# A hybrid attention and delta-rule layer on one core: when the second half's input block is prepared, and how the diagonal blocks travel

## The chip, the cores and the metric

The kernel runs on one core of one Trainium2 chip. Its engines are TensorE (PE, with its weight loads PEld), VectorE (DVE), ScalarE (ACT), GpSimd (POOL) and SyncE (SP), whose queue issues the kernel's DMA transfers. Each engine works through its own list of instructions in order. The metric is the device time of one execution in microseconds; three runs of the kernel before took 1336.61, 1340.53 and 1341.32 us, with the median 1340.53.

## The reference, cut to what matters

One layer takes x (2048 positions of 1024 numbers), normalises it, projects it once, and gives the columns to two groups: a gated delta rule that scans the sequence in both directions (4 heads of 128, chunks of 64) and attention in a band of 128 positions to either side (8 query heads over 2 key/value heads of 64). The outputs are concatenated, projected and added to x.

```python
h = rms_norm(x, norm_w[l])
proj = h @ w_in[l]
(dn_q, dn_k, dn_v, dn_z, dn_beta, dn_decay,
 sw_q, sw_k, sw_v, sw_z) = jnp.split(proj, cuts, axis=-1)
dn = gated_deltanet_bidir(dn_q, dn_k, dn_v, dn_beta, dn_decay,
                          dn_conv_w[l], dn_a_log[l], dn_dt_bias[l])
dn = rms_norm(dn, dn_out_norm_w[l]).reshape(b, s, DN_WIDTH)
dn = dn * jax.nn.silu(dn_z)
sw = windowed_gqa_with_sinks(sw_q, sw_k, sw_v, ...)
sw = sw * jax.nn.silu(sw_z)
x = x + jnp.concatenate([dn, sw], axis=-1) @ w_out[l]
```

Inside the delta rule each chunk needs the inverse of a unit lower triangular matrix:

```python
m = jnp.where(strict, jnp.einsum('bhncd,bhnsd->bhncs', k_beta, k) * decay, 0.0)
eye = jnp.eye(c, dtype=q.dtype)
t_inv = lax.linalg.triangular_solve(eye + m, jnp.broadcast_to(eye, m.shape),
                                    left_side=True, lower=True, unit_diagonal=True)
u = jnp.einsum('bhncs,bhnse->bhnce', t_inv, v * beta[..., None])
w = jnp.einsum('bhncs,bhnsd->bhncd', t_inv, k_beta * jnp.exp(g)[..., None])
def step(state, inp):
    v_new = u_i - jnp.einsum('bhcd,bhde->bhce', w_i, state)
    ...
```

## The kernel before, in words

The sequence is cut into 16 chunks of 128 positions, and into four blocks of 512, two to a half. A float32 product is made of three products of rounded parts (xhi, xlo for the input; wh, wl for a weight).

**Phase A** goes through the two halves. In each half it prepares the input blocks (`xprep` L145 to L165 writes xhi and xlo, whose tiles have two buffers: the second half's first block, xhi2, takes the buffers of the first half's first block), then projects keys, values and queries of the attention (`proj_seq` L191, tiles pq), the gates (`gate_pairs` L202, tiles pf_z, twice 128 channels at a time), and the channels of the delta rule with their convolution (`conv_pair` L217, tiles pf_c: ACT makes the first tap at L233, DVE the other four at L237). Between these pieces of projection it does the attention of one chunk after the other (`attend` L327): PE scores s (L339, L340), DVE the masked maximum (L341), ACT the exponential (L346), POOL the division (L355), PE transposes (L360), ACT and DVE split the result in two parts (L364, L365), PE multiplies with the values (L367, L368), ACT and DVE put the output together in ot (L371 to L374), POOL multiplies with the gate zc and SP stores it as mix_sw (L375 to L378). ot5_1 is the output of chunk 5, the sixth, for the second key/value head.

**Phase B** begins while the last attention is under way. `out_sw` (L564) projects the attention's part of the output chunk by chunk (pcs, with weights that ACT and DVE split into wohs and wols, L542, L543; xrs is the residual that DVE adds, L561). For each of the four heads h there is `pre_front(h)` (L604), which makes the chunk matrices ma from the keys and stores them in DRAM (m_d, L675) in four groups of four chunks, in the order 1, 2, 0, 3; `pre_back(h)` (L689), which loads the 32 x 32 diagonal blocks of all chunks and both directions into L0 and L (L697, L698; a partition for each block), copies L0 into L (L700), solves them all at once in 31 steps of two instructions on DVE (L705, L709; the result is X), stores X as x_d (L710), reloads it in pieces xc in the layout of the chunk matrices (L718), transposes (xt, L719), copies it to its places on POOL (iv L724 to L728, ma L745) and builds each full inverse by products pi (L733); and `scan(h)` (L759), which steps through the chunks in both directions with kqc loads (L771, four buffers) ahead of it. `out_dn` (L865) projects the second part of the output at the end.

**The order** on each engine isn't the order of the program. `set_order` (L884) builds a graph of the instructions with what each one reads and writes, gives each a cost, and plans a list for every engine by repeated forward and backward list scheduling. Its `gate(before, after)` (L984) adds a node to that graph: everything in `after` is planned behind everything in `before`. A gate puts no wait on the chip; it only changes the lists, and all buffers and semaphores follow from them. Tiles that take turns in a buffer are gated in this way anyhow.

## Time and profile before

| | |
|---|---|
| median of three runs | 1340.53 us |
| the profiled execution | 1339.74 us |
| its span on the core | 1338.0 us |
| mean granted clock of PE | 0.979 |
| first chunk's first scores (s0_0) | 169 us |
| last matmul of the first half's projections (z15_0_1) | 332 us |
| last matmul of the second half's projections (z15_1_1) | 724 us |
| last matmul of out_sw | 893 us |
| last reciprocal blocks stored (x_d of head 3) | 1160 us |

A row of a view by stage has the window, its length, the busy time of each engine with the number of instructions in brackets, then the granted clock of PE, the busy share of the DMA engines, and GB/s. A row of the timeline has its start, its duration, the engine, the line, the operation with out<-in, and in square brackets the idle time before it with what ended it. Rows on DMA issues have count, size, and the median time from issue to landing. In the chain of waits a row is start, duration, engine, tile and line. Tile names stand without their numbers in all of these, so that L0 and L are both L, and which chunk or head a row belongs to follows from its time and its place in the order.

### The profile page before, as it was taken

How to read it: one execution, taken by the hardware profiler on the slowest of the kernel's cores; microseconds unless marked ns; L12 is line 12 of the kernel's file. 1: busy time of each engine (PE TensorE's matmuls, PEld its weight loads, DVE VectorE, ACT ScalarE, POOL GpSimd, SP SyncE). 2: the span in 40 equal slices, each digit the busy share in tenths (PEclk: the TensorE clock that was granted, in tenths of full speed). 3: DMA queues.
4: the chain of work that ended last, by engine and by line, in shares of the span. 5: the costliest groups of instructions: out<-in, count | busy, mean ns of one | idle time of the engine just before them, and what ended most of it. 6: DMA issues, size and time to landing. Idle time of an engine off the chain costs nothing.

```text
span 1338.0 us, 22553 instructions
## 1 busy us (share of the span) xinstructions
PE 1258.0 (94%) x7162; PEld 1072.9 (80%) x7162; DVE 885.6 (66%) x2250; ACT 711.3 (53%) x2105; POOL 484.4 (36%) x868
## 2 busy tenths in 40 slices
PE   5999999999999999999999899998979879898998
PEld 4998878788998888888888687778868769788776
DVE  4423387773632399999987899666885877846433
ACT  5422264332433467666667877229868766466310
POOL 1223032100021235755786755228238155170000
PEclk8999999999999999999999999999979989989999
DMA  7442345244443533222334757968567274333776
GB/s 235 135 140 78 104 161 171 73 135 135 148 121 114 163 102 109 72 93 83 96 120 130 249 185 226 291 209 217 144 184 207 84 212 104 94 104 106 233 241 209
DMA packets 219686, 201.16 MB, mean 150 GB/s; under 512 B 48304, under 2 KB 170800, under 8 KB 219568
## 3 DMA queue, kind: packets, MB, share of 16 engines
q1 hardware_dynamic: 219568, 199.73, 48.8%
q8 instruction: 57, 0.93, 0.3%
q14 instruction: 61, 0.50, 0.1%
HBM read 134.59 MB, written 65.08 MB: 149 GB/s over the span
## 4 chain that ended last, share of the span: by engine, by line
PE 72%; DVE 9%; DMA 5%; ACT 5%; POOL 5%; issue 3%; SPq 0%; DVEq 0%; POOLq 0%; ACTq 0%
PE pf_c L186 6%; PE pf_c L187 6%; PE pf_c L188 5%; PE pf_z L186 4%; PE pf_z L187 4%; PE pf_z L188 4%; PE pi L733 4%; PE pt L360 2%; PE pq_q L197 2%; PE pq_q L199 2%; PE pq_q L198 2%; PE pcd L559 2%; PE pcd L560 2%; PE pcd L558 2%; PE pcs L558 2%
## 5 line engine op out<-in xcount | busy, mean ns | idle before, releaser
L237 DVE SCALAR_TENSOR_TENSOR acc<-pf_c,cw,acc 128x512 f32<-128x512 f32 (+1 forms) x192 | 140.0, 745 | 22.7 <-ACT acc L233 20.9
L186 PE MATMUL pf_c<-xhi,wh_c 128*128 128x512 f32 x384 | 149.3, 401 | 1.9 <-DVE acc L237 1.1
L187 PE MATMUL pf_c<-xlo,wh_c 128*128 128x512 f32 x384 | 150.4, 401 | 0.0
L188 PE MATMUL pf_c<-xhi,wl_c 128*128 128x512 f32 x384 | 148.4, 400 | 0.0
L186 PE MATMUL pf_z<-xhi,wh_z 128*128 128x512 f32 x256 | 91.6, 400 | 0.1
L355 POOL TENSOR_SCALAR pr<-pr,st 128x384 f32<-128x384 f32 (+1 forms) x128 | 83.5, 670 | 22.5 <-DVE st L353 19.0
L187 PE MATMUL pf_z<-xlo,wh_z 128*128 128x512 f32 x256 | 91.0, 397 | 0.0
L346 ACT ACTIVATE pr<-pr,st 128x384 f32<-128x384 f32 (+1 forms) x128 | 76.2, 598 | 27.3 <-DVE st L345 26.7
L188 PE MATMUL pf_z<-xhi,wl_z 128*128 128x512 f32 x256 | 90.3, 396 | 0.0
L186 PEld LDWEIGHTS pf_c<-xhi,wh_c 128*128 128x128 f32 x384 | 72.3, 189 | 17.5 <-DVE acc L237 1.9
L188 PEld LDWEIGHTS pf_c<-xhi,wl_c 128*128 128x128 f32 x384 | 72.0, 188 | 14.6
L187 PEld LDWEIGHTS pf_c<-xlo,wh_c 128*128 128x128 f32 x384 | 72.3, 188 | 13.9
L341 DVE CUSTOM_DVE_ANT_0 pr<-s,mask,sink 128x384 f32<-128x384 f32 (+1 forms) x128 | 72.6, 594 | 6.0 <-PE pt L360 2.5
L360 PE MATMUL pt<-ident,pr 128*128 128x128 f32 x368 | 72.8, 276 | 3.3 <-ACT q L323 1.4
L364 ACT ACTIVATE ph<-pt 128x512 fp32r<-128x512 f32 x92 | 53.4, 594 | 40.2 <-PE pt L360 37.3
L365 DVE TENSOR_TENSOR pl<-pt,ph 128x512 fp32r<-128x512 f32 x92 | 62.5, 684 | 9.1 <-ACT ph L364 7.9
L670 DVE SCALAR_TENSOR_TENSOR ma<-gh,bp,dc 128x256 f32<-128x256 f32 x128 | 56.1, 476 | 17.7 <-PE gh L661 10.0
L787 ACT ACTIVATE yk<-py,ck 128x128 f32<-128x128 f32 x120 | 44.0, 367 | 40.4 <-PE py L782 39.1
L360 PEld LDWEIGHTS pt<-ident,pr 128*128 128x128 f32 x368 | 48.6, 141 | 19.2 <-POOL pr L355 4.8
L178 DVE TENSOR_TENSOR wl_c<-ws_c,wh_c 128x512 fp32r<-128x512 f32 x48 | 36.6, 765 | 37.0 <-ACT wh_c L177 24.7
L197 PE MATMUL pq_q<-wh_q,xhi 128*128 128x256 f32 x256 | 58.5, 284 | 0.8 <-ACT sgq L256 0.8
L561 DVE TENSOR_TENSOR xrd<-xrd,pcd 128x512 f32<-128x512 f32 x32 | 20.9, 684 | 55.5 <-PE pcd L560 55.5
(250 smaller groups left out, 3769.9 us busy)
## 6 DMA issues: line engine op xcount, KB each, us to landing
kqc<-kq_d SPq DMA_DIRECT2D x120, 128.0 KB, 2.5
ws_c<-wt SPq DMA_DIRECT2D x48, 256.0 KB, 3.5
xr<-x SPq DMA_DIRECT2D x16, 512.0 KB, 6.0
ws_z<-wt SPq DMA_DIRECT2D x32, 256.0 KB, 3.4
kq<-kq_d SPq DMA_DIRECT2D x16, 512.0 KB, 4.9
xrs<-x SPq DMA_DIRECT2D x32, 256.0 KB, 3.4
part<-xrs SPq DMA_DIRECT2D x32, 256.0 KB, 3.4
m_d<-ma SPq DMA_DIRECT2D x32, 256.0 KB, 4.9
```

What stands on the lines that cost most here:

```text
L186: T.matmul(ps, hi[:, k, cs], xhi[b][:, k], start=(k == 0), stop=False)
L187: T.matmul(ps, hi[:, k, cs], xlo[b][:, k], start=False, stop=False)
L188: T.matmul(ps, lo[:, k, cs], xhi[b][:, k], start=False, stop=(k == KC - 1))
L197: T.matmul(ps[:, :n], xh, hi[:, k, :n], start=(k == 0), stop=False)
L237: V.scalar_tensor_tensor(av, ps[:, lo:], cw[:, i, k : k + 1], av, ALU.mult, ALU.add)
L341: V.tensor_tensor_reduce(pr[j][:, :n], ps[:, :n], mask[:, lo * P : hi * P], 1.0, sink[:, hh : hh + 1], ALU.add, ALU.max, accum_out=mx[:, j ...
L346: A.activation(pr[j][:, :n], pr[j][:, :n], AF.Exp, bias=nm[:, j : j + 1], accum_out=den[:, j : j + 1])
L355: G.tensor_scalar(pr[j][:, :n], pr[j][:, :n], den[:, j : j + 1], 1.0, ALU.mult, ALU.mult)
L360: T.transpose(pt[:, j], pr[j][:, (kb - lo) * P : (kb - lo + 1) * P], ident)
L365: V.tensor_tensor(pl, ptf, ph.bitcast(F32), ALU.subtract)
L558: T.matmul(ps, mh[:, k], wh[:, k, ns], start=(k == 0), stop=False)
L670: V.scalar_tensor_tensor(ma[d, c4][:, c], gh[:, k], bp[:, d, cc : cc + 1], gms[d][:, c : c + 1].to_broadcast([P, 2, P]), ALU.mult, ALU.mult,)
```

## The change

Two things are changed. First, the planner gets one more gate: all instructions that use xhi2 (its preparation and the projections that read it) are planned behind all that use ot5_1. Second, the chunk matrices of a group get a DRAM tile of their own, so that the diagonal blocks are loaded group by group, in pieces of 16 partitions, inside `pre_front`, and X is stored in three pieces (16, 16 and 96 partitions) instead of one: the first two hold the blocks that the first products need, and the first reloads read only those. There are 32 loads of L instead of 8 and 12 stores of x_d instead of 4, 32 more instructions on SP (876 to 908); the instructions of the other engines are the same in number and kind, in another order.

```diff
@@ pre_front
-        m_d = dp.tile([2, NCH, 4 * (32 * P + 32)], F32, tag="m_d", name=f"m_d{h}", bufs=2)
-        x_d = dp.tile([2, NCH, P, 32], F32, tag="x_d", name=f"x_d{h}", bufs=2)
+        L0 = qp.tile([64, 32, 32], F32, tag="L0", name=f"L0{h}")
+        L = qp.tile([P, 32, 32], F32, tag="L", name=f"L{h}")
+        x_d = [dp.tile([4 * n, P, 32], F32, tag=f"x_d{j}", name=f"x_d{h}_{j}", bufs=2) for j, n in enumerate((1, 1, 6))]
...
+            m_d = dp.tile([2, 4, 4 * (32 * P + 32)], F32, tag=f"m_d{n}", name=f"m_d{h}_{c4}", bufs=2)
             for d in range(2):
-                dma(m_d[d, s4, : P * P].rearrange("u (i j) -> i u j", j=P), ma[d, c4][:, :, 0])
+                dma(m_d[d, :, : P * P].rearrange("u (i j) -> i u j", j=P), ma[d, c4][:, :, 0])
+            for d in range(2):
+                lv = m_d[d].rearrange("u (p y) -> (u p) y", p=4)[:, : 32 * P]
+                lo = 64 * d + 16 * c4
+                dma((L if d else L0)[lo : lo + 16], lv.rearrange("q (r x) -> q r x", x=P)[:, :, :32])
@@ pre_back
-        lv = [m_d[d].rearrange("u (p y) -> (u p) y", p=4)[:, : 32 * P] for d in range(2)]
-        lv = [a.rearrange("q (r x) -> q r x", x=P)[:, :, :32] for a in lv]
-        dma(L0, lv[0])
-        dma(L[64:128], lv[1])
...
-        dma(x_d.rearrange("d u (p r) c -> (d u p) (r c)", p=4), X.rearrange("p r c -> p (r c)"))
+        for a, lo, hi in zip(x_d, (0, 112, 16), (16, 128, 112)):
+            dma(a.rearrange("u (p r) c -> (u p) (r c)", p=4), X[lo:hi].rearrange("p r c -> p (r c)"))
...
-                dma(xc, x_d[d, 4 * c4 : 4 * c4 + 4].rearrange("u i c -> i u c"))
+                lo = 4 * (3 * d + c4 - 1 + d)
+                dma(xc, (x_d[2][lo : lo + 4] if hi else x_d[d]).rearrange("u i c -> i u c"))
@@ set_order
+    second = [k for x in used if x.startswith("xhi2_") for k in used[x]]
+    for x in used:
+        if x.startswith("ot5_1_"):
+            gate(used[x], second)
```

What the gate does to PE shows at the edge between the halves. Names there: pf_z15_0_1 is the last z projection of the first half, s and pt are scores and transposes of the chunk in the name (s1_0: chunk 1, head 0), ptq transposes its queries, and pq_kv8 is the first projection of the second half. PE before:

```order
L187 MATMUL pf_z15_0_1_4187<-xlo1_220,wh_z14_0_3939 128x512
L188 MATMUL pf_z14_0_1_4160<-xhi1_219,wl_z14_0_3940 128x512
L188 MATMUL pf_z15_0_1_4187<-xhi1_219,wl_z14_0_3940 128x512
L339 MATMUL s1_0_1871<-k2_147,q2_1_0_1475 128x384
L339 MATMUL s1_1_1877<-k2_147,q2_1_0_1475 128x384
L340 MATMUL s1_0_1871<-k2_147,q2_1_0_1475 128x384
L340 MATMUL s1_1_1877<-k2_147,q2_1_0_1475 128x384
```

PE at the same edge now:

```order
L187 MATMUL pf_z15_0_1_4187<-xlo1_220,wh_z14_0_3939 128x512
L188 MATMUL pf_z14_0_1_4160<-xhi1_219,wl_z14_0_3940 128x512
L188 MATMUL pf_z15_0_1_4187<-xhi1_219,wl_z14_0_3940 128x512
L339 MATMUL s6_0_3764<-k2_147,q2_6_0_3390 128x384
L340 MATMUL s6_0_3764<-k2_147,q2_6_0_3390 128x384
L339 MATMUL s6_1_3770<-k2_147,q2_6_0_3390 128x384
L340 MATMUL s6_1_3770<-k2_147,q2_6_0_3390 128x384
```

Before, the second half began with chunk 1's scores; now chunks 1 to 5 are done and chunk 6 begins. By the softmax instructions (L341, 16 to a chunk) on DVE, 180 of 256 stood ahead of the last z result of the second half before, and 202 do now. The first half's pairs c2/c3, c6/c7 and c10/c11 have 6, 0 and 0 before, and 24, 24 and 16 now; the second half's pairs that end with c5, c9, c3, c7 and c11 have 32, 24, 20, 20 and 24 before, and 0, 0, 2, 12 and 32 now. Up to chunk 0's output sum, chunk 2's and chunk 5's, the tail has 24, 16 and 36 before, and 16, 14 and 24 now.

On DVE the place of head 0's solve moves. xrs8_1 is the second sum of chunk 8 in out_sw, mls a part of the next chunks, L0_9535 the tile L of head 0, tm and X the solve's steps. DVE before:

```order
L561 TENSOR_TENSOR xrs8_0_9216<-xrs8_0_9216,pcs8_0_9218 128x512
L561 TENSOR_TENSOR xrs8_1_9233<-xrs8_1_9233,pcs8_1_9235 128x512
L700 COPY L0_9535<-L00_9534 64x1024
L551 TENSOR_TENSOR mls10_9293<-mxs10_9290,mhs10_9292 128x512
L705 TENSOR_TENSOR tm0_0_9541<-L0_9535,X0_9536 128x31
L709 TENSOR_TENSOR X0_9536<-X0_9536,tm0_0_9541 128x31
```

DVE now:

```order
L561 TENSOR_TENSOR xrs9_1_9288<-xrs9_1_9288,pcs9_1_9290 128x512
L551 TENSOR_TENSOR mls12_9388<-mxs12_9385,mhs12_9387 128x512
L561 TENSOR_TENSOR xrs10_0_9311<-xrs10_0_9311,pcs10_0_9313 128x512
L561 TENSOR_TENSOR xrs10_1_9328<-xrs10_1_9328,pcs10_1_9330 128x512
L700 COPY L0_8582<-L00_8581 64x1024
L705 TENSOR_TENSOR tm0_0_9552<-L0_8582,X0_9549 128x31
```

The solve stands two chunks of out_sw later. On SP the store and the reloads of head 1's inverses (x_d1, xc1) stand among the loads for the scan (kqc1) and the stores of the next head's matrices (m_d2). SP before:

```order
L710 DMA x_d1_10619<-X1_10932 128x1024
L771 DMA kqc1_0_4_11445<-kq_d1_88 128x2x128
L771 DMA kqc1_1_4_11466<-kq_d1_88 128x2x128
L675 DMA m_d2_12014<-ma2_2_12027 128x4x128
L621 DMA kq2_3_12248<-kq_d2_89 128x2x512
L718 DMA xc1_0_0_11031<-x_d1_10619 128x4x32
```

SP now:

```order
L711 DMA x_d1_0_10633<-X1_10958 16x1024
L711 DMA x_d1_1_10634<-X1_10958 16x1024
L632 DMA dc2_0_1_12213<-gr_d_5033 128x4x128
L711 DMA x_d1_2_10635<-X1_10958 96x1024
L773 DMA kqc1_1_3_11451<-kq_d1_88 128x2x128
L773 DMA kqc1_0_4_11471<-kq_d1_88 128x2x128
L773 DMA kqc1_1_4_11492<-kq_d1_88 128x2x128
L720 DMA xc1_0_0_11057<-x_d1_0_10633 128x4x32
```

Four rows stand between store and first reload before, six now, two of them the other pieces. And this is SP where head 3's block loads (L03, L3) follow the stores of their groups (m_d3), among head 2's reloads (xc2), now:

```order
L677 DMA m_d3_0_13680<-ma3_3_13625 128x4x128
L720 DMA xc2_0_2_12600<-x_d2_2_12044 128x4x32
L681 DMA L03_13449<-m_d3_0_13680 16x32x32
L681 DMA L3_13450<-m_d3_0_13680 16x32x32
L720 DMA xc2_1_1_12604<-x_d2_2_12044 128x4x32
L677 DMA m_d3_3_13759<-ma3_3_13625 128x4x128
L720 DMA xc2_0_3_12667<-x_d2_2_12044 128x4x32
```

Before, all loads of a head's blocks stood behind its last m_d store.

More of the change, by code (lines that the diff above doesn't have):

```diff
@@ L684, in pre_front @@
             V.tensor_tensor(ck[:, d], bp[:, d], ekd[:, d, :, h], ALU.mult)
-        H["solve"] = m_d, x_d, mp
+        H["solve"] = L0, L, x_d, mp
         return H
@@ L690, in pre_back @@
         ma = H["ma"]
-        m_d, x_d, mp = H["solve"]
-        L0 = qp.tile([64, 32, 32], F32, tag="L0", name=f"L0{h}")
-        L = qp.tile([P, 32, 32], F32, tag="L", name=f"L{h}")
+        L0, L, x_d, mp = H["solve"]
         X = qp.tile([P, 32, 32], F32, tag="X", name=f"X{h}")
-        lv = [m_d[d].rearrange("u (p y) -> (u p) y", p=4)[:, : 32 * P] for d in range(2)]
-        lv = [a.rearrange("q (r x) -> q r x", x=P)[:, :, :32] for a in lv]
-        dma(L0, lv[0])
-        dma(L[64:128], lv[1])
         dma(X, t["eye32"].partition_broadcast(P))
```

## The prediction

> **What bounds the kernel now.** I read the page's head first, then busy time by stage, then the waits and the chain where the stages change, and last the DMA issues.
>
> ```profile
> span 1338.0 us, 22553 instructions
> PE 1258.0 (94%) x7162; PEld 1072.9 (80%) x7162; DVE 885.6 (66%) x2250; ACT 711.3 (53%) x2105; POOL 484.4 (36%) x868
> ```
>
> The profiled execution took 1339.74 us around this span and the median of the runs is 1340.53, so a sum made against the profile is read 0.8 us higher for the median. PE is the bound on average. The change gives PE the same instructions in another order, so a gain can only come from places where PE stands still or is held to another engine's pace. The next table is by stage; the edges are ends of a channel pair's last matmul (c7 and c11 of the first half, then c9, c3, c7, c11 of the second).
>
> ```profile
> core 0: us, PE busy (x) PEld busy (x) DVE busy (x) ACT busy (x) POOL busy (x), PEclk, DMA share, GB/s
> 244.00:266.20 22.20, 22.20 (x98) 18.04 (x97) 15.37 (x21) 5.83 (x9) 2.54 (x8) 1.00 0.30 102
> 266.20:287.70 21.50, 21.50 (x95) 17.50 (x94) 15.57 (x21) 6.80 (x11) 0.25 (x3) 1.00 0.30 98
> 517.00:552.10 35.10, 35.10 (x181) 28.83 (x180) 32.71 (x85) 24.64 (x63) 22.62 (x33) 1.00 0.30 95
> 552.10:586.40 34.30, 34.30 (x181) 28.51 (x180) 32.90 (x89) 25.47 (x61) 26.41 (x39) 1.00 0.33 106
> 586.40:620.50 34.10, 34.10 (x173) 28.11 (x172) 32.18 (x78) 22.48 (x52) 17.97 (x31) 1.00 0.29 94
> 620.50:655.40 34.90, 34.90 (x181) 29.14 (x180) 33.20 (x85) 23.07 (x55) 21.51 (x32) 1.00 0.28 87
> ```
>
> A pair without attention takes 21.9 us (mean of two) with DVE at 15.5 and ACT at 6.3. A pair with attention takes 34.6 (mean of four), DVE 32.7, ACT 23.9. DVE's order holds 88 softmax instructions (L341) in those four stages; a chunk has 16, so a stage carries 1.375 chunks. One chunk then costs (34.6-21.9)/1.375 = 9.3 us of a stage, (32.7-15.5)/1.375 = 12.6 of DVE and 12.8 of ACT. DVE would set the pace once 15.5+12.6a exceeds 21.9+9.3a, at a = 1.9 chunks per pair. Behind the last z projection (724) the kernel is no longer so smooth:
>
> ```profile
> 724.10:762.30 38.20, 31.41 (x166) 23.33 (x165) 32.82 (x95) 33.89 (x108) 23.54 (x34) 0.96 0.83 262
> 762.30:784.30 22.00, 21.71 (x114) 17.77 (x113) 20.25 (x56) 15.55 (x41) 16.11 (x20) 1.00 0.53 175
> 784.30:827.60 43.30, 42.82 (x242) 35.69 (x241) 41.15 (x138) 33.44 (x110) 18.88 (x29) 1.00 0.71 213
> ...
> PE pcs L558 <- ACT wohs L542: 1.4, 2, 0.9
> ...
> 751.59 0.82 DVE wols L543
> ```
>
> PE stands still for 6.8 of 38.2 us, ACT is busy 33.9 of them, and the chain of waits runs through ACT and the conversion of the output weights (wohs, wols). In the third row DVE is busy 41.2 of 43.3 us. This tail is held by ACT and DVE, and it is where less attention would help.
>
> **The change, part by part.** *The gate.* It has no work of its own. By DVE's order, of the 256 softmax instructions 180 stood ahead of the last z result before and 202 do now; 54 instead of 76 are left for the tail. So 22, or 1.375 chunks, leave the tail. The first half's pairs c3, c7, c11 now carry 1.5, 1.5 and 1.0 chunks, the second half's c5, c9, c3, c7, c11 carry 0, 0, 0.1, 0.75 and 2.0. Only the last reaches 1.9, by a hair, so I charge each moved chunk 9.3 us where it goes: phase A grows by 1.375 x 9.3 = 12.8. The tail loses 1.375 x 12.6 = 17.3 if DVE sets its pace and 12.8 if PE does. The net by load is 0 to -4.5. The first tail stage also has the 6.8 us of standing still, behind a queue on ACT that becomes half a chunk shorter (24 to 16 softmax instructions up to its end, 0.5 x 12.8 = 6.4 us of ACT, of which 4.7 are counted with the chunk). I take -7, with ends 0 and -9.
>
> At the new edge between the halves, the input block's preparation and the key/value weights stand in the queues behind the sixth chunk's last store.
>
> ```profile
> ws_kv<-wkv SPq DMA_DIRECT2D x8, 136.0 KB, 3.7
> m_d<-ma SPq DMA_DIRECT2D x32, 256.0 KB, 4.9
> L<-m_d SPq DMA_DIRECT2D x8, 256.0 KB, 4.5
> x_d<-X SPq DMA_DIRECT2D x4, 512.0 KB, 4.3
> xc<-x_d SPq DMA_DIRECT2D x32, 64.0 KB, 2.9
> ```
>
> PE has the rest of the z projections and the seventh chunk's scores to do meanwhile. One weight load lands in 3.7 us; uncovered, it and its conversion would cost about 4 (estimate from that row). I take +1, ends 0 and +4.
>
> *The diagonal blocks.* 24 more L loads and 8 more x_d stores, all on SP; nothing is added on another engine. Head 0 is where the order moves against the change:
>
> ```profile
> 852.87 0.69 DVE L561 TENSOR_TENSOR xrs<-xrs,pcs 128x512 f32<-128x512 f32 x1 [1.35 <-PE pcs L560]
> 853.48 1.12 DVE L700 COPY L<-L 64x1024 f32<-64x1024 f32 x1
> 855.11 0.20 DVE L705 TENSOR_TENSOR tm<-L,X 128x31 f32<-128x31 f32 x1
> ...
> 888.13 0.33 SPq L710 DMA_DIRECT2D x_d<-X  x1
> ...
> 893.86 0.69 DVE L561 TENSOR_TENSOR xrs<-xrs,pcs 128x512 f32<-128x512 f32 x1 [0.44 <-PE pcs L560]
> ...
> 896.16 2.08 PE L733 MATMUL pi<-iv,g 128*128 128x128 f32 x8 [2.33 <-POOL iv L724]
> ```
>
> The first solve takes 33 us (855.1 to 888.1) beside the output projection. It began after chunk 8's residual sum; now it begins after chunk 10's. Seven chunks, 8 to 15, take 41.0 us (852.9 to 893.9), so two are 11.7 us. The solve was done 5.7 us ahead of the last sum; it will be done 6.0 after it, less two chunks' DVE work beside it (4 sums and 2 splits of about 0.69 = 4.1), so some 2 after. From its end to the first product it took 8.0 us, and the early pieces cut that. PE, which paused 2.3 us here, would pause about 8, so the uncovered price is 5 to 7. What PE can't do here is the next head's front, which runs then and isn't left for later; I let about half come back: +3, ends 0 and +7.
>
> Heads 1 to 3:
>
> ```profile
> 986.79 0.33 SPq L710 DMA_DIRECT2D x_d<-X  x1
> 992.73 0.37 SPq L718 DMA_DIRECT2D xc<-x_d  x1
> 996.55 0.61 POOL L724 COPY iv<-xc 32x128 f32<-32x128 f32 x2 [1.89 <-DMA xc<-x_d]
> ...
> 1082.76 0.46 SPq L710 DMA_DIRECT2D x_d<-X  x1
> 1089.13 0.92 SPq L718 DMA_DIRECT2D xc<-x_d  x2
> ...
> 1092.71 1.65 POOL sso L829
> ...
> 1160.03 0.34 SPq L710 DMA_DIRECT2D x_d<-X  x1
> 1166.55 2.19 SPq L718 DMA_DIRECT2D xc<-x_d  x4
> 1168.73 0.61 POOL L724 COPY iv<-xc 32x128 f32<-32x128 f32 x2 [10.61 <-DMA xc<-x_d]
> ...
> PE pi L733 <- POOL iv L724: 3.7, 2, 2.3
> PE tr L641 <- DMA kq<-kq_d: 2.7, 2, 1.5
> ```
>
> From store to first reload it takes 5.9, 6.4 and 6.5 us, and POOL waits for the reload. A piece of 16 partitions holds 64 KB; the nearest row of that size, xc, lands in 2.9 against 4.3, so each head gains 1.4 if the reload follows at once, 4.2 in all. In head 2 the copies now also stand ahead of the square-root step on POOL (1.65). Against that, the list of PE's waits (the two last lines: us in all, times, longest) has 3.7 us for these copies, of which 2.3 are head 0's: in heads 1 to 3 PE mostly waits for other things, and an earlier inverse helps only as far as those allow. I take -4 in all. If the reloads followed a 2.9 us landing everywhere, 3.0 + 3.5 + 3.6 = -10 is the far end; three stores at 0.3 to 0.5 each in front of it, gaining nothing, is about +3.
>
> The Trainium skill ("DMA: Bandwidth & Descriptors", Anatomy of one DMA) puts a transfer at about 2.0 us plus its bytes at 436 GB/s and says the fixed part is mostly the wait for completion. By it 64 KB would be estimated at 2.15 us and 512 KB at 3.2, a gain of 1.05 a head in place of 1.4, and the heads about -3; the rows here lie above it in both sizes.
>
> **Sum.** -7 + 1 + 3 - 4 = -7: 1332.7 against the profile, 1333.5 against the median. I say 1333.
>
> **Rivals.** *A. Given back.* The tail's gain stays at the load's 4.5, PE pays 6 at head 0, and the early pieces give 2.5 since other reloads stand between: -4.5+1+6-2.5 = 0, 1340. For it: many waits beside the one removed; against it: POOL's 10.6 and 1.9 us of waiting for exactly this reload.
>
> *B. The early store does nothing* (its reloads stand behind stores, scan loads and block loads in SP's order): -7+4 = -3, 1337.
>
> *C. SP's queue becomes the bound, and the kernel is slower.* Each block load waits for its group's m_d store to land, and SP goes on with nothing else meanwhile.
>
> ```profile
> 847.68 3.11 SPq L698 DMA_DIRECT2D L<-m_d  x1
> ...
> 960.00:1000.00 40.00, 31.74 (x171) 25.55 (x170) 34.76 (x125) 26.58 (x127) 10.98 (x17) 0.81 0.61 172
> ```
>
> In heads 1 to 3 there are 12 pairs of block loads instead of 3. By SP's order two to twelve rows stand between a group's last store and its load; at about 0.4 us a row (0.33 to 0.46 above) that covers 0.8 to 4.8 of the 4.9 us. In head 3 two rows stand between one store and its load, and the other reloads of head 2 are queued behind them. Nine added pairs at some 2.5 us are 22 us of SP; it decides from the point where a stop outlasts the loads that the scan has in hand (four buffers). If two thirds of it reached PE, +15: 1347; with the issue itself at 3.1 us, as in the row, up to 1355. Against it: in before SP already stops for stores in this way, and the only DMA that PE is shown to wait for more than once is kq, 2.7 us (the last line above).
>
> *D. The clock.* In 960:1000 PE is idle for 8.3 us and the granted clock is 0.81 over 40 us, a loss of 7.6. If head 0's longer pause brought such a stage: -7+1+7+7.6-4 = +4.6, 1345. The Trainium skill ("TensorE: Matmul & The Clock Gate", Part 1) has the clock halved after an idle window of about 3.4 us, which speaks for this; the clock in that row agrees that pauses cost more than themselves.
>
> **How the numbers follow.** A measurement of this kernel can tell about 0.5% from no change, 6.7 us: faster is below 1333.8, slower above 1347.2. My forecast, with all sums that gain more than 6.7: 0.46, on the edge of what counts as faster. Same: A 0.17, B 0.09, D 0.05, 0.31 together. Slower: C 0.19 and several terms at their bad ends 0.04, 0.23 together. All good ends give -19 (1321), all bad ends +14 (1354). Leaving one in ten out on either side gives 1322 to 1349; the forecast's own range is 1325 to 1338.
>
> **What would show it.** Right: softmax work in 215 to 345 and little in 420 to 520; from the last z result to chunk 5's output sum (103.5 us now) about 84; the first product of head 0 some 5 us later behind the last output sum; from x_d to the first xc under 5 us in heads 1 to 3. Wrong: the tail as long as before less 12.8, PE waiting for DVE in first-half pairs, gaps in PE that end with kqc, or a clock under 0.9 near head 0.

## The result and the profile after

The changed kernel takes 1345.58 us (median of nine runs, 1342.67 to 1350.32) against 1341.05 for the kernel before (nine runs): the ratio is 1.0047 with the interval 1.0029 to 1.0065. It is slower by about half a per cent. The forecast was 1333 us, 0.5% faster.

The profiled execution took 1349.31 us, among the slower of its runs, and 9.6 more than that of before; the sums of stages below are of these two executions. The head of the page after:

```profile
span 1347.3 us, 22603 instructions
PE 1259.6 (93%) x7162; PEld 1072.4 (80%) x7162; DVE 883.2 (66%) x2250; ACT 713.8 (53%) x2105; POOL 479.6 (36%) x868
```

Busy times are the same within 5 us, so the time is in pauses. The next fence is busy time by stage after, with columns as in the prediction's table: first half c7 and c11; second half c7, c11, both z pairs; the tail up to chunks 0, 2 and 5 of the output; the rest of the output projection; and 20 us behind it.

```profile
250.20:284.40 34.20, 34.20 (x176) 28.26 (x175) 32.37 (x83) 23.05 (x57) 20.70 (x32) 1.00 0.28 92
284.40:320.90 36.50, 36.50 (x189) 30.24 (x188) 35.54 (x87) 25.90 (x64) 24.82 (x39) 1.00 0.30 93
593.90:621.00 27.10, 27.10 (x131) 22.32 (x129) 23.72 (x49) 13.27 (x26) 4.03 (x6) 1.00 0.28 88
621.00:662.40 41.40, 41.24 (x217) 33.66 (x216) 39.22 (x106) 30.63 (x76) 27.09 (x42) 1.00 0.26 85
662.40:704.20 41.80, 40.93 (x216) 33.29 (x216) 35.16 (x94) 29.44 (x72) 33.64 (x43) 1.00 0.29 97
704.20:739.30 35.10, 34.38 (x177) 27.97 (x176) 29.51 (x87) 24.68 (x64) 28.99 (x47) 1.00 0.25 83
739.30:770.70 31.40, 26.19 (x130) 18.79 (x129) 25.13 (x72) 29.09 (x94) 17.19 (x20) 0.95 0.83 267
770.70:789.90 19.20, 18.96 (x102) 15.66 (x101) 17.69 (x56) 13.28 (x36) 8.38 (x11) 1.00 0.55 181
789.90:828.00 38.10, 37.33 (x198) 30.07 (x197) 31.04 (x99) 22.93 (x72) 12.83 (x22) 1.00 0.67 210
828.00:899.70 71.70, 64.66 (x277) 51.59 (x277) 42.84 (x97) 16.25 (x51) 13.10 (x14) 0.95 0.83 254
899.70:920.00 20.30, 12.39 (x65) 9.75 (x64) 11.61 (x41) 11.37 (x55) 9.41 (x28) 0.75 0.69 190
```

And the last two of these stages in the kernel before:

```profile
827.60:893.40 65.80, 62.24 (x274) 49.13 (x273) 49.14 (x116) 16.26 (x42) 14.82 (x21) 1.00 0.83 264
893.40:913.70 20.30, 16.02 (x106) 14.01 (x106) 9.33 (x31) 15.04 (x73) 16.55 (x50) 0.92 0.61 153
```

The attention did move: first-half pairs take 34 to 37 us, and the tail is 88.7 us instead of 103.5. But the last z result comes 15.2 us later (739.3 for 724.1), and at chunk 5's output sum the kernels are level, 828.0 and 827.6. Then the rest of the output projection takes 71.7 instead of 65.8, and in the 20 us behind it PE is busy for 12.4 instead of 16.0, at a granted clock of 0.75 instead of 0.92. That is where the time is lost.

The rows of the timeline around the first solve after, with two of the waits of DVE and PE there:

```profile
DVE xrs L561 <- DMA xrs<-x: 10.4, 4, 6.1
PE pcs L558 <- DVE xrs L561: 5.7, 3, 3.8
...
871.44 0.69 DVE L561 TENSOR_TENSOR xrs<-xrs,pcs 128x512 f32<-128x512 f32 x1 [6.09 <-DMA xrs<-x]
872.04 1.04 DVE L700 COPY L<-L 64x1024 f32<-64x1024 f32 x1
905.17 1.26 SPq L711 DMA_DIRECT2D x_d<-X  x3
905.37 1.02 POOL L652 TENSOR_TENSOR nk<-ssk,pw 128x4 f32<-128x4 f32 x1 [42.05 <-DVE ssk L651]
907.14 0.99 SPq L720 DMA_DIRECT2D xc<-x_d  x2
907.62 1.11 PE L642 MATMUL tr<-ident,kq 128*128 128x128 f32 x4 [3.85 <-ACT vs L688]
915.55 1.12 PE L735 MATMUL pi<-iv,g 128*128 128x128 f32 x8
```

In the kernel before, the two waits were these:

```profile
DVE xrs L561 <- DMA xrs<-x: 1.3, 2, 1.1
PE pcs L558 <- DVE xrs L561: 1.8, 2, 1.3
```

So DVE waits longer for residual loads, and PE longer for DVE. The inverses are stored at 905.2, 17 us later than before (888.1) and 5.5 behind the end of the output projection, where before it was 5.3 ahead. The first product follows at 915.6, for 896.2. The next head's front can't fill the pause, since its first step on DVE (ssk) stands behind the solve in DVE's list, and POOL (nk) and ACT (vs) follow from that.

In heads 1 to 3, store and first reload after:

```profile
996.97 0.98 SPq L711 DMA_DIRECT2D x_d<-X  x2
1002.44 0.55 SPq L720 DMA_DIRECT2D xc<-x_d  x1
...
1090.73 0.96 SPq L711 DMA_DIRECT2D x_d<-X  x2
1096.22 0.59 SPq L720 DMA_DIRECT2D xc<-x_d  x1
...
1169.00 2.45 SPq L711 DMA_DIRECT2D x_d<-X  x3
1174.42 0.38 SPq L720 DMA_DIRECT2D xc<-x_d  x1
...
L<-m_d SPq DMA_DIRECT2D x32, 64.0 KB, 5.0
x_d<-X SPq DMA_DIRECT2D x8, 64.0 KB, 3.2
```

Store and first reload stand 5.5, 5.5 and 5.4 us apart, for 5.9, 6.4 and 6.5 before. The last two rows give count, size and median landing time of the block loads and of the two small pieces of X.

### The profile page after: what moved, and what is told of

It is laid out like the page before. It is cut to its first block, busy times and chain, and to the rows that moved or that the text cites. A ratio compares the mean times of both kernels' runs of the same rounds, so it can differ in the third digit from the quotient of the medians.

```text
span 1347.3 us, 22603 instructions
## 1 busy us (share of the span) xinstructions
PE 1259.6 (93%) x7162; PEld 1072.4 (80%) x7162; DVE 883.2 (66%) x2250; ACT 713.8 (53%) x2105; POOL 479.6 (36%) x868
## 5 line engine op out<-in xcount | busy, mean ns | idle before, releaser
L237 DVE SCALAR_TENSOR_TENSOR acc<-pf_c,cw,acc 128x512 f32<-128x512 f32 (+2 forms) x192 | 140.6, 745 | 26.1 <-ACT acc L233 24.5
L355 POOL TENSOR_SCALAR pr<-pr,st 128x384 f32<-128x384 f32 (+1 forms) x128 | 83.4, 670 | 80.0 <-DVE st L353 56.6
L346 ACT ACTIVATE pr<-pr,st 128x384 f32<-128x384 f32 (+1 forms) x128 | 76.3, 598 | 40.2 <-DVE st L345 37.3
L187 PE MATMUL pf_z<-xlo,wh_z 128*128 128x512 f32 x256 | 95.3, 402 | 0.0
L188 PE MATMUL pf_z<-xhi,wl_z 128*128 128x512 f32 x256 | 94.6, 400 | 0.0
L341 DVE CUSTOM_DVE_ANT_0 pr<-s,mask,sink 128x384 f32<-128x384 f32 (+1 forms) x128 | 73.1, 593 | 13.3 <-PE s L340 9.4
L365 DVE TENSOR_TENSOR pl<-pt,ph 128x512 fp32r<-128x512 f32 x92 | 62.2, 682 | 10.6 <-ACT ph L364 9.7
L233 ACT ACTIVATE acc<-pf_c,cw 128x512 f32<-128x512 f32 x48 | 32.7, 682 | 53.7 <-PE pf_c L188 53.6
L558 PE MATMUL pcs<-wohs,mhs 128*128 128x512 f32 x128 | 54.0, 425 | 6.3 <-DVE xrs L561 5.7
```

What stands on the lines that cost most here:

```text
L187: T.matmul(ps, hi[:, k, cs], xlo[b][:, k], start=False, stop=False)
L188: T.matmul(ps, lo[:, k, cs], xhi[b][:, k], start=False, stop=(k == KC - 1))
L237: V.scalar_tensor_tensor(av, ps[:, lo:], cw[:, i, k : k + 1], av, ALU.mult, ALU.add)
L341: V.tensor_tensor_reduce(pr[j][:, :n], ps[:, :n], mask[:, lo * P : hi * P], 1.0, sink[:, hh : hh + 1], ALU.add, ALU.max, accum_out=mx[:, j ...
L346: A.activation(pr[j][:, :n], pr[j][:, :n], AF.Exp, bias=nm[:, j : j + 1], accum_out=den[:, j : j + 1])
L355: G.tensor_scalar(pr[j][:, :n], pr[j][:, :n], den[:, j : j + 1], 1.0, ALU.mult, ALU.mult)
```

## The experiments

For comparing kernels I use, beside times, the PE time lost: the time from one matmul to another less the sum of the spacings that their pairs of shapes have in the trace of before in the median. It takes the moved work out of a stage's length. It is a sum from one profiled execution each, good to a few us. One spacing has to be read with care: the step from the last output matmul straight to the first product occurs once in the kernel before, with 2.8 us, so this counts there as the usual spacing. The pause before reads as 0, though PE stands still for 2.3 us in it, and kernels without a pause read -2.5. The table gives it from the start up to an event (us), with the time from the last output matmul to the store of head 0's inverses (negative: stored earlier) and the chunk of the output projection behind which the solve stands in DVE's list.

```
                       last z  chunk 5  out_sw  first    scan 0  end of   x_d less   solve
                       result  output   end     product  done    scans    out_sw end behind
before                  46.8    67.6     73.5    73.5     90.6    157.8     -5.3      8
changed                 50.7    68.2     79.6    91.3    105.7    170.7     +5.5     10
e1 gate                 46.5    73.8     77.2    74.7     92.7    159.7    -10.7      7
e2 diagonal part        49.4    70.8     79.4    90.0    109.6    172.3     +5.1     11
e3 gate, loads          48.3    67.9     79.5    86.0    100.6    169.1     +2.5      9
e4 gate, split          49.3    76.6     84.9    82.4    104.1    168.4    -12.1      6
e5 split                46.7    72.7     76.7    74.2     96.1    159.8     -9.0      8
e6 loads                47.6    72.2     81.9    89.3    107.9    170.0     +2.8     10
e7 changed, head 0 whole 47.9   68.6     76.1    73.6     92.4    160.0    -10.7      7
e8 changed, early solve 52.5    69.1     80.0    85.1    103.0    160.9     -1.9      8
e9 changed, front late  46.0    69.0     73.0    95.3    109.4    171.7    +16.5     11
e10 e8 and e9           49.1    63.7     68.5    76.0     93.5    155.2     -2.0      8
e11 before, tail moved  45.1    59.0     68.0    76.4     93.3    145.6     +3.9     10
e12 heads 1 to 3        46.7    73.5     75.4    72.9     90.7    158.3    -10.3      7
e13 changed, tail moved 48.6    63.8     78.2    97.6    112.4    179.2    +10.6     11
e14 e10 and e13         48.0    63.2     66.0    73.3     88.9    148.4     -2.6      8
e15 e11, early solve    49.5    67.4     71.7    69.2     84.8    146.8    -14.8      6
```

Medians and ratios stand with each run below; the kernel before beside them had medians of 1338.28 to 1340.57.

### The parts apart (e1 to e6)

e1 is the kernel before with the gate alone:

```diff
+    second = [k for x in used if x.startswith("xhi2_") for k in used[x]]
+    for x in used:
+        if x.startswith("ot5_1_"):
+            gate(used[x], second)
```

> The gate alone, with the diagonal blocks as in the kernel before. Theory 1 (the loads by group are what costs: they make the out projection slower and put the first solve later): the stretch from chunk 5's output sum to the last output matmul is 66 us as before, the first product of head 0 follows 0 to 5 us behind it, and the time is 1334 to 1340. Theory 2 (the gate itself costs: the later attention meets the out projection, and its residual loads are late): that stretch is 70 or more, and the time is 1343 to 1348.

Measured: 1343.43, ratio 1.0033 (1.0019 to 1.0047). The pause is gone as theory 1 says, but the time isn't. By DVE's order this kernel still has 76 softmax instructions in its tail, as many as before: the gate by itself takes none out. What it does is an exchange inside phase A, and the tail loses 6 us more than before, of which 2 to 3 come back in the rest of the output projection.

e2 leaves the gate out and keeps the rest:

```diff
-    second = [k for x in used if x.startswith("xhi2_") for k in used[x]]
-    for x in used:
-        if x.startswith("ot5_1_"):
-            gate(used[x], second)
```

> The diagonal blocks by group and the early pieces, without the gate. Theory 1: the first product of head 0 comes 13 us or more behind the last output matmul (its solve now stands behind chunk 11's first sum), and the time is 1345 to 1352. Theory 2: the pause is a few us and the time is 1336 to 1341.

Measured: 1353.69, ratio 1.0112 (1.0077 to 1.0146), with 10.6 us lost in the pause. Theory 1 holds here: the diagonal part costs, and costs more without the gate.

e3 is the changed kernel with one store of X and its reloads as before:

```diff
-        for a, lo, hi in zip(x_d, (0, 112, 16), (16, 128, 112)):
-            dma(a.rearrange("u (p r) c -> (u p) (r c)", p=4), X[lo:hi].rearrange("p r c -> p (r c)"))
+        dma(x_d.rearrange("d u (p r) c -> (d u p) (r c)", p=4), X.rearrange("p r c -> p (r c)"))
```

> Gate and loads by group, but X stored by one transfer. Theory 1: as the changed kernel or some 3 us slower, 1345 to 1350, with heads 1 to 3 no faster than before. Theory 2: 1343 to 1348 as well, so this run tells what the pieces of x_d are worth, not the two theories.

Measured: 1345.92, ratio 1.0050 (1.0029 to 1.0070), the same as the changed kernel. So the pieces of the store are worth nothing there that can be told.

e4 is e1 (the kernel before with the gate) with the pieces added, and the block loads as before:

```diff
-        dma(x_d.rearrange("d u (p r) c -> (d u p) (r c)", p=4), X.rearrange("p r c -> p (r c)"))
+        for a, lo, hi in zip(x_d, (0, 112, 16), (16, 128, 112)):
+            dma(a.rearrange("u (p r) c -> (u p) (r c)", p=4), X[lo:hi].rearrange("p r c -> p (r c)"))
...
-                dma(xc, x_d[d, 4 * c4 : 4 * c4 + 4].rearrange("u i c -> i u c"))
+                lo = 4 * (3 * d + c4 - 1 + d)
+                dma(xc, (x_d[2][lo : lo + 4] if hi else x_d[d]).rearrange("u i c -> i u c"))
```

> Gate and early pieces of x_d, with the loads of the blocks as before, behind a head's last store. Theory 1: no slow stretch in the out projection, the pause before head 0 at most 3 us, heads 1 to 3 some 3 us shorter, 1331 to 1338. Theory 2: 1342 to 1347.

Measured: 1349.48, ratio 1.0080 (1.0054 to 1.0107). A miss: the pause is gone, but the tail and the first scan lose more. Theory 1 doesn't cover this kernel.

e5 is the kernel before with the same pieces and without the gate:

```diff
-        dma(x_d.rearrange("d u (p r) c -> (d u p) (r c)", p=4), X.rearrange("p r c -> p (r c)"))
+        for a, lo, hi in zip(x_d, (0, 112, 16), (16, 128, 112)):
+            dma(a.rearrange("u (p r) c -> (u p) (r c)", p=4), X[lo:hi].rearrange("p r c -> p (r c)"))
...
```

> The kernel before with X stored in three pieces and nothing else of the change. If the pieces help as I reckoned (1 to 2 us a head from the store to the first product), the time is 1334 to 1338; if their reloads only wait for other things, 1339 to 1342. If three stores in SP's queue cost by themselves, 1343 or more.

Measured: 1342.78, ratio 1.0024 (1.0014 to 1.0033). Not a gain, but a small loss.

e6 is the kernel before with the loads by group alone:

```diff
+            m_d = dp.tile([2, 4, 4 * (32 * P + 32)], F32, tag=f"m_d{n}", name=f"m_d{h}_{c4}", bufs=2)
...
+            for d in range(2):
+                lv = m_d[d].rearrange("u (p y) -> (u p) y", p=4)[:, : 32 * P]
+                lo = 64 * d + 16 * c4
+                dma((L if d else L0)[lo : lo + 16], lv.rearrange("q (r x) -> q r x", x=P)[:, :, :32])
```

> The kernel before with the blocks loaded by group and nothing else. Theory now: the loads by group are what puts head 0's solve two chunks of the out projection later, so PE pauses some 10 us before head 0's first product, and the stretch behind chunk 5's output sum loses 3 to 6 us more than before: 1345 to 1352. Rival (the pause comes from the attention that the gate moved): pause under 4 us, 1338 to 1342.

Measured: 1350.51, ratio 1.0082 (1.0060 to 1.0105), pause 7.4, the out projection's rest 9.7 lost for 5.9. The loads by group alone make both losses. No gate is needed for them.

### Head 0 (e7 to e10)

e7 is the changed kernel with head 0's blocks loaded as before, in two loads behind its last store:

```diff
+            if h == 0:
+                for d in range(2):
+                    dma(m_0[d, s4, : P * P].rearrange("u (i j) -> i u j", j=P), ma[d, c4][:, :, 0])
+                for d in range(2) if n == 3 else ():
+                    lv = m_0[d].rearrange("u (p y) -> (u p) y", p=4)[:, : 32 * P]
+                    dma((L if d else L0)[64 * d : 64 * d + 64], lv.rearrange("q (r x) -> q r x", x=P)[:, :, :32])
+            else:
...
```

> The changed kernel with head 0's blocks loaded as before (two loads behind the last store of its matrices); heads 1 to 3 by group. Head 0's solve then stands behind chunk 7's sum instead of chunk 10's. If the late solve of head 0 is what the change pays for, the pause before head 0's first product falls from 12 us of lost PE time to 0 to 3, and the time is 1336 to 1341. If not, 1344 to 1348.

Measured: 1339.75, ratio 0.9994 (0.9971 to 1.0016): the whole loss is gone. The copy ahead of the solve, the store and the first product in its timeline:

```profile
847.63 1.12 DVE L709 COPY L<-L 64x1024 f32<-64x1024 f32 x1
886.27 0.80 SPq L720 DMA_DIRECT2D x_d<-X  x2
897.24 1.05 PE L744 MATMUL pi<-iv,g 128*128 128x128 f32 x8
```

The copy is 24 us earlier than in the changed kernel and PE goes from the last output matmul (897.0) straight to the product.

e8 keeps the loads by group and only has the planner put the solve earlier:

```diff
+    first_solve = [k for k in used[next(x for x in used if x.startswith("tm0_0_"))]]
+    for x in used:
+        if x.startswith("pcs9_0_"):
+            gate(first_solve, [k for k in used[x] if insts[k][1] == "DVE"])
```

> The changed kernel with one more planner gate: head 0's first solve step is planned ahead of chunk 9's output sum, so that the solve starts behind chunk 8's, as before; the blocks are still loaded by group. If the place of the solve is the cause, the pause falls by 6 to 10 us and the time is 1336 to 1341. If the loads' waits in SP's queue are the cause, the out projection stays 3 to 6 us slower than before and the time is 1342 to 1348.

Measured: 1343.48, ratio 1.0031 (1.0017 to 1.0044). In between: the pause's loss falls from 11.7 to 5.1, and the output projection still loses 10.9 (11.4 in the changed kernel). The place of the solve accounts for part of the loss; what keeps the projection slow, this run doesn't tell.

e9 holds back loads of the next head's front that the changed kernel issues during the output projection:

```diff
+    last_res = [k for x in used if x.startswith(("xr15_1_", "xrs15_1_")) for k in used[x][:1]]
+    for x in used:
+        if x.startswith(("kq1_2_", "vt1_2_", "dc1_2_0_", "dc1_2_1_")):
+            gate(last_res, [k for k in used[x] if insts[k][1] == "SP"])
```

> The changed kernel with the loads of the next head's second group (keys, values, decays: some 1.3 MB) planned behind the last residual load of the out projection. In the changed kernel DVE waits 10 us for residual loads there, with the DMA engines busy all the time. If those extra loads are the cause, the stretch from chunk 5's output sum to the last output matmul loses 6 us of PE time or less, as before, instead of 11.5, while the pause before head 0 stays, 1340 to 1344. If SP's waits for the block loads are the cause, it still loses 9 to 12 and the time is 1344 to 1349.

Measured: 1354.62, ratio 1.0111 (1.0074 to 1.0148). The mechanism came as expected, the time did not. DVE's wait for residual loads is 1.8 us for 10.4:

```profile
DVE xrs L561 <- DMA xrs<-x: 1.8, 1, 1.8
...
871.40 1.08 DVE L700 COPY L<-L 64x1024 f32<-64x1024 f32 x1
909.74 1.51 SPq L711 DMA_DIRECT2D x_d<-X  x3
924.10 1.23 PE L735 MATMUL pi<-iv,g 128*128 128x128 f32 x8
...
893.20:924.10 30.90, 14.37 (x58) 9.80 (x57) 20.26 (x57) 17.34 (x80) 12.37 (x23) 0.78 0.63 189
```

The output projection loses 4.0 us and ends 6.5 us earlier than in the changed kernel, at 893.2; the solve comes no earlier, so the pause is 30.9 us. With the projection over earlier, more of the chain from the solve to the first product lies open, and that chain is longer too: 14.4 us from store to product, for 10.4. e10 is the changed kernel with the gates of e8 and e9 together:

```diff
+    last_res = [k for x in used if x.startswith(("xr15_1_", "xrs15_1_")) for k in used[x][:1]]
...
+            gate(last_res, [k for k in used[x] if insts[k][1] == "SP"])
+    first_solve = [k for k in used[next(x for x in used if x.startswith("tm0_0_"))]]
...
+            gate(first_solve, [k for k in used[x] if insts[k][1] == "DVE"])
```

> Both remedies on the changed kernel: the early first solve and the next head's second group behind the residual loads. If each works by itself, 1336 to 1341; if the loads by group keep the DMA engines busy anyhow, 1342 to 1346.

Measured: 1336.22, ratio 0.9980 (0.9963 to 0.9996). With both, the changed kernel is as fast as the one before, or a trifle faster.

### The tail and all together (e11 to e15)

e11 is the kernel before with one gate, which puts more attention ahead of the last z projection and does nothing else:

```diff
+    last_z = [k for x in used if x.startswith(("z15_1_1_", "pf_z15_1_1_")) for k in used[x]]
+    for x in used:
+        if x.startswith("ot12_0_"):
+            gate(used[x], last_z)
```

> The kernel before with one planner gate that puts the attention up to the first half of chunk 12 ahead of the last z projection: 40 softmax instructions are left for the tail instead of 76, and nothing else is changed. My forecast's term by load: 36 instructions are 2.25 chunks, 2.25 x (12.6-9.3) = 7 us off the sum of phase A and tail, 1330 to 1335. The rival: what the tail gives, the stages that take the chunks lose, 1338 to 1343, or more where the first solve is put later too (it stands behind chunk 10's sum).

Measured: 1330.49, ratio 0.9939 (0.9918 to 0.9959): 8 us. Up to chunk 5's output it is 6.2 us ahead of the kernel before, for 7 by the term, so the term by load holds there. The time doesn't come from that alone: in the profiled executions its first product is 7.4 us later than before and its end 12.3 earlier, so nearly 20 us come back in the heads. That execution is the fastest of its ten, at a granted clock of 0.995 (0.979 in the kernel before's); how much of this is the clock isn't shown. By DVE's order the planner put 58 softmax instructions beside the second half's first projections, where there had been 6:

```profile
416.50:486.10 69.60, 69.60 (x353) 57.70 (x352) 49.52 (x125) 47.10 (x126) 49.63 (x68) 1.00 0.46 142
743.10:783.10 40.00, 34.21 (x192) 25.75 (x191) 35.25 (x111) 37.66 (x129) 12.26 (x16) 1.00 0.85 276
783.10:798.50 15.40, 15.40 (x77) 12.66 (x76) 11.03 (x37) 7.82 (x23) 4.74 (x7) 1.00 0.61 190
798.50:821.40 22.90, 22.90 (x113) 19.01 (x112) 16.14 (x43) 8.53 (x21) 5.61 (x10) 1.00 0.74 234
```

DVE is at 71% in the first row, so PE sets the pace there, and the last two rows have no idle PE. In the changed kernel, by contrast, 78 softmax instructions stand in the second half's c11 and the two z pairs behind it; in c11 DVE is busy for 39.2 of 41.4 us (the table of after).

e12 is the kernel before with loads by group and pieces in heads 1 to 3 alone; head 0 is as before, and there is no gate:

```diff
+            if h == 0:
...
+                for d in range(2) if n == 3 else ():
+                    lv = m_0[d].rearrange("u (p y) -> (u p) y", p=4)[:, : 32 * P]
+                    dma((L if d else L0)[64 * d : 64 * d + 64], lv.rearrange("q (r x) -> q r x", x=P)[:, :, :32])
+            else:
...
+                    lo = 64 * d + 16 * c4
+                    dma((L if d else L0)[lo : lo + 16], lv.rearrange("q (r x) -> q r x", x=P)[:, :, :32])
...
+        cuts = ((0, 16), (112, 128), (16, 112)) if h else ((0, 128),)
+        for a, (lo, hi) in zip(x_d, cuts):
+            dma(a.rearrange("u (p r) c -> (u p) (r c)", p=4), X[lo:hi].rearrange("p r c -> p (r c)"))
```

> The kernel before, without the gate and with head 0 as it was: loads by group and early pieces for heads 1 to 3 alone. If those are worth 3 to 4 us in all, as I reckoned, 1335 to 1339; if they are worth nothing, 1339 to 1342; if the twelve pairs of loads stop SP's queue, 1344 or more.

Measured: 1340.35, ratio 1.0010 (0.9993 to 1.0026): nothing. Neither the gain I reckoned nor the stop in SP's queue.

e13 adds the gate of e11, these same lines, to the changed kernel:

```diff
+    last_z = [k for x in used if x.startswith(("z15_1_1_", "pf_z15_1_1_")) for k in used[x]]
+    for x in used:
+        if x.startswith("ot12_0_"):
+            gate(used[x], last_z)
```

> The changed kernel with the planner gate that puts the attention up to the first half of chunk 12 ahead of the last z projection; 40 softmax instructions are left for the tail instead of 54, and the second half's last pairs carry at most 24. The solve of head 0 stands behind chunk 11's first sum. If only the crowded stages cost the gain, the lost PE time up to chunk 5's output sum falls by 5 to 9 us and the time is 1337 to 1342. If head 0's late solve decides, what is won there is lost in the pause (14 us or more), and the time is 1343 to 1350.

Measured: 1356.41, ratio 1.0108 (1.0075 to 1.0141). The loss up to chunk 5's output falls from 68.2 to 63.8, and the pause takes it back several times over: 19.4 lost, with the store 10.6 us behind the output projection. The time lies outside both ranges. e14 is e10 with that gate too, so the changed kernel with three gates more:

```diff
+            gate(used[x], last_z)
...
+            gate(last_res, [k for k in used[x] if insts[k][1] == "SP"])
...
+            gate(first_solve, [k for k in used[x] if insts[k][1] == "DVE"])
```

> The changed kernel with all three remedies: the attention out of the tail, the first solve behind chunk 8's sum, the next head's second group behind the residual loads. If the costs found are the whole of it, 1328 to 1333; if the loads by group or the gate cost something else, 1336 or more.

Measured: 1331.31, ratio 0.9922 (0.9892 to 0.9951), as expected; faster than both kernels. It is no faster than e11, which has the last gate and nothing of the change, so even without its losses the change adds nothing to that gate that can be told. Its stages from the last z result on:

```profile
746.20:783.80 37.60, 32.11 (x172) 23.71 (x171) 32.52 (x100) 33.10 (x105) 12.32 (x15) 1.00 0.90 285
783.80:800.50 16.70, 16.35 (x87) 13.47 (x86) 12.87 (x40) 9.71 (x28) 5.99 (x9) 1.00 0.65 208
800.50:827.20 26.70, 26.70 (x131) 21.81 (x130) 18.41 (x48) 11.59 (x44) 9.40 (x15) 1.00 0.90 278
827.20:886.30 59.10, 56.45 (x253) 45.93 (x251) 40.07 (x95) 9.84 (x27) 4.34 (x4) 1.00 0.83 258
```

The last row is the one that took 71.7 us in the changed kernel; it still has the gate and the whole diagonal part. e15 is e11 with the early solve of e8:

```diff
+            gate(used[x], last_z)
...
+            gate(first_solve, [k for k in used[x] if insts[k][1] == "DVE"])
```

> The kernel before, without the diagonal part, with the attention out of the tail and the first solve planned early (it then stands behind chunk 6's sum). If the two add up, 1324 to 1331; if the earlier solve slows the output projection by what it saves in the pause, 1330 to 1335.

Measured: 1334.46, ratio 0.9955 (0.9938 to 0.9971). No better than e11 (1330.49). With the solve behind chunk 6 the pause is gone, and the first product comes 8.5 us earlier than in e11 (895.1 for 903.6), although 8.4 us more are lost up to chunk 5's output, 4.4 of them ahead of the last z result. The gain is gone again behind it: by the table heads 1 to 3 lose 62.0 us, for 52.3 in e11. Why they do is not shown. So taking the pause away isn't a gain by itself.

## Why the prediction was wrong

The spans of the two profiled executions differ by 9.3 us, and the differences of stage lengths give it (a scan ends here with its last product): 0.4 up to chunk 5's output, 5.9 for the rest of the output projection, 13.1 in the pause, -8.0 of it back by the end of scan 0, and -2.1 in heads 1 to 3. I had forecast -7 for the first of these, +3 for the pause and what comes back, -4 for the heads, and nothing for the projection.

**The tail, -7 with ends 0 and -9: the step that failed first.** It came out as 0. Of the 7.4 us that are missing, 2.4 are phase A's, which grew by 15.2 instead of 12.8, and 5.0 are the tail's, which took 88.7 us instead of the 84 that I had named. For the tail I priced the chunks that leave at DVE's pace (17.3) and added part of the standing still; my own terms gave 6.2 at that end, and I took 7. What came is near PE's price. In the tail's last stage DVE is busy for 31.0 of 38.1 us now (41.2 of 43.3 before) and PE for 37.3, so DVE no longer sets the pace there; in the first stage PE still stands still for 5.2 us of the 6.8. PE's price of 12.8 and these 1.6 make 14.4 of the 14.8 us by which the tail is shorter (an estimate from these rows, not tested by a run). My own sign of being wrong, "the tail as long as before less 12.8", would be 90.7.

In phase A the charge of 9.3 wherever a chunk goes was wrong: c11 of the second half, with 2.0 chunks, lost 3.5 us of PE time (1.8 before), and the two z pairs behind it 4.1 and 3.6 (2.4 and 1.6). I checked the limit of 1.9 chunks for c11 alone and called it "by a hair"; for the z pairs I worked out none. In e11, which puts its chunks elsewhere, a moved chunk costs phase A 8.4 us and gives the tail 11.2; in the changed kernel it costs 11.1 and gives 10.8. And I put the shift down to the gate. e1 shows that the gate leaves the tail's 76 softmax instructions where they were; the shift came out of the plan for both parts together.

**The output projection: no term at all, +5.9.** I had priced what the loads by group do on SP in heads 1 to 3 (rival C), and nothing beside the output projection. There PE's waits for the residual sums went from 1.8 to 5.7 us, DVE's for residual loads from 1.3 to 10.4, and the granted clock from 1.00 to 0.95, with the DMA engines about as busy as before (0.83 in both rows). e9, e10 and e14, which plan 1.3 MB of the next head's loads behind this stretch, lose 4.0, 4.8 and 2.8 us in it, for 11.4. So in these kernels the place of those loads decides. It isn't the whole cause: e6 loses 9.7 there with 0.3 us of this wait, and e11, with the block loads as before, loses 9.0 with 6.7.

**Head 0, +3 with ends 0 and +7.** The net is 5.1, within its ends, from larger parts: 13.1 of pause for the 5 to 7 that I had, and 8.0 returned for about half. That these come out near my figure is luck. I put the solve's end 2 us behind the projection; the store was 5.5 behind it. And I had the early pieces cut the 8.0 us from store to first product; it took 10.4 (6.8 in e3, with one store). The reading that the solve's place decides the pause is borne out by e7, e8 and the table: where the store is 9 us or more ahead of the projection's end, the pause loses nothing; 5.3 us ahead, in the kernel before, PE stands still for 2.3; 2.6 ahead to 5.5 behind, it loses 5 to 12 us; 10.6 and 16.5 behind, 19 and 22. The pause alone doesn't decide the time: e11 loses 8.4 us in it and is faster than the kernel before; e1, e4 and e5 have none and are slower.

**Heads 1 to 3, -4.** The stages give -2.1: -6.5 in head 1, and +0.9 and +3.5 in heads 2 and 3. Store and reload came 0.4 to 1.1 us closer, 2.4 in all for 4.2, and e5 and e12 gained nothing. The claim that the gap would be under 5 us was wrong. The 64 KB stores landed in 3.2 us, not 2.9, and six rows of SP's list stand between. What I overlooked is when the solve ends. In the eleven kernels that store X in pieces, head 3's inverses go out 6.7 to 7.5 us ahead of the last product of head 2's scan, and from there to head 3's last product it takes 83.5 to 87.9 us; in the six with one store they go out 9.2 to 10.5 us ahead, and it takes 80.5 to 84.0. So with the pieces head 3 is about 3 us longer. Why the plan ends the solve later there is not shown.

The Trainium skill ("DMA: Bandwidth & Descriptors", Anatomy of one DMA) fits the formula that I cited to transfers issued from GpSimd; the ones here are issued from SP. Its difference of 1.05 us between the two sizes is near the 1.1 between the landing times (4.3 us for 512 KB, 3.2 for 64 KB), and both times lie about 1.1 us above it.

**The edge between the halves, +1.** Nothing: PE waits 0.7 us at the first projections of the second half, for 0.5 before.

**The rivals.** C's slower end is not what happened: from the first to the last product with a kqc load, the scans of heads 1 to 3 took 69.8, 59.4 and 55.5 us, for 71.9, 60.2 and 56.6, so no stop of SP lengthened them. A, the gain given back at head 0, is nearest to what came: it has 6 there (net 5.1) and 2.5 for the pieces (2.1), but it too counts on 4.5 from the tail, and has nothing for the projection. D's 1345 is within a us of the result, and that is luck: its sum keeps the -7 of the tail, and pays 14.6 us at head 0 where the net is 5.1. The clock that it names was there: 0.75 over the 20 us of the pause, in which PE stands still for up to 3.85 us at a time, and this agrees with the Trainium skill's halving after an idle window ("TensorE: Matmul & The Clock Gate", Part 1). It is 5.1 us of clock for D's 7.6. No rival named a cost in the output projection.

**What stays open.** Why the plan puts head 0's matrices and its last store later when the blocks are loaded by group. In the changed kernel the last store was issued at 855.2 us, 16 later than before, behind chunk 8's output stores in SP's list; e7 shows that one change of those loads undoes it, not which of the planner's rules did it. Also open is why e4 loses in the tail and in scan 0, and where e11 gains in the heads. Every gate and every other way of loading gave a new order on all engines, so no run changes one thing alone.

## What to carry to other kernels

Work that is taken out of a crowded stretch may have been the cover of a chain of latencies beside it. Before it is moved, write down when the chain's last step could end and when the cover ends, and treat the difference as a stock that the change spends. Here the store came 5.3 us ahead of the cover's end, but the chain ran on for 8.0 us to the first product: the stock was already spent, and PE stood still for 2.3 us.

A priority gate in a planner, or other loads, moves everything near it, so the effect of one edit is read from the new order and not from the edit. Gating exactly the work that should move (e11) gave all that the change with three more gates gave (e14). Charge moved work at the pace of the stage that receives it and credit it at the pace of the stage that gives it up, and ask in each which engine will set the pace after the move.

## What the runs showed of the hardware

A quarter of a load wasn't quicker than the whole. The block loads of 64 KB landed in 5.0 us in the median, those of 256 KB in 4.5; the same 128-byte pieces went in 32 loads instead of 8. Over the other runs with 32 such loads the median is 4.3 to 5.0, over those with 8 it is 4.5 to 5.1.

The granted clock falls where PE stands still, but not in proportion: 0.92 over 20 us with PE busy for 16.0 (before), 0.75 over 20 us with 12.4 (after), 0.78 over 31 us with 14.4 (e9). And it can't be charged one for one: over the 76 runs of the kernel before that were measured beside the experiments, a straight line through time and lost clock (one less the granted clock, times the time) gives about 0.4 us for each us lost, with a wide scatter.
